# Delta-rule mixer: a head's transposes, norms and decayed keys become a step of their own, called right behind the head's projections

## The chip, the cores and the metric

The kernel runs on one core of a Trainium2 chip. The metric is the device time of one execution in microseconds (us). The engines are named as the profile names them: PE is TensorE, DVE is VectorE, ACT is ScalarE, POOL is GpSimd, SP is SyncE, whose queue issues nearly all DMAs. Each engine runs its own instructions in a fixed order. An instruction that waits for another engine holds up everything behind it on its own engine.

## The reference

Two model blocks run one after the other on 512 tokens of width 1024. The change lies in the first block's mixer, which has a gated delta rule (4 heads of 128) beside a retention (4 heads of 128). For each delta-rule head the reference computes:

```
qkv = silu(causal_dwconv(concat(q, k, v), conv_w))     # 4 taps
q, k = l2norm(q) * d**-0.5, l2norm(k)                  # per token
beta = sigmoid(b);  g = -exp(a_log) * softplus(a + dt_bias);  gcum = cumsum(g) in a chunk
m = tril(kb @ k.T * decay, -1);  t_mat = inverse(I + m);  qk = q @ k.T * decay
u = t_mat @ vb - (t_mat @ (kb * exp(gcum))) @ state
o = (q * exp(gcum)) @ state + qk @ u
state = state * exp(gcum[-1]) + (k * exp(gcum[-1] - gcum)).T @ u
out = rms(o) * norm_w * silu(gate)
```

The rest of the program is an MLP with a convolution, a window attention, an MLP, a differential attention and an MLP.

## The kernel before

All matrices are held with features on the partitions and the 512 tokens on the free axis. A projection gives one 128x512 tile: weights and activations are split into two fp32r halves, and each of the 8 slices of the contraction takes three matmuls (xh x hi, xl x hi, xh x lo), so a tile has 24 matmuls of 128x512 (`project`, PSUM buffers `ps_pj`, 3 of them). The weights come in blocks of 1 MB on SP's queue. ACT makes the high half of a block (L251), DVE the low half (L252); each half has four buffers. All other PSUM tiles share five buffers (`pwt`).

In the mixer, `conv_silu` takes a projected tile from PSUM to `cs` (DVE L556, times the row norm), starts the convolution on ACT (`cy`, L558), adds three taps on DVE (L560) and applies silu on ACT (L562) into `kT`, `KQ[:, 1]` or `vT`. The buffers of `cy` are a pair that is shared with `er` below.

`stage_a(hh)` prepares one head. Its first half makes the token-major copies of k and q by four PE transposes each (`ps_kt`), takes eight squares with a sum on ACT (`junk`, `ssq`), runs `col_rsqrt` (twelve small DVE instructions, three rounds of Newton, L400 to L410), and scales the result (`rkq`, `brk`, `kdc`). Its second half broadcasts `brk` by eight small matmuls (`ps_bc`), multiplies k by it (`KQ[:, 0]`, L590), forms the decay (`ps_gr`, then `E` on DVE, exp to `E` and `er` on ACT, four POOL operations to `E`, `E2`, `qd`, `kbe`), takes the Gram matrices (`ps_gram`, then `N` and `QE` on DVE, L622), sends `N` to DRAM, makes the decayed keys `kd` from the transposed keys that still lie in PSUM (L627), and the token-major values `vb` (`ps_vt`, L634). `stage_b1` inverts the 16x16 blocks of N on DVE (`pr`, `tt`), `stage_b2` builds the whole inverse (`ps_X`, `ps_T`, `ps_U`), `stage_c` runs the recurrence over four chunks for two heads and ends with a norm (POOL L795 on `o`). `finish` transposes `o` (`ps_oT`) and applies the gate.

The order of the calls is: k and q of heads 0, 1; the decay columns; v of heads 0, 1; `stage_a(0)`, `stage_a(1)`; k and q of heads 2, 3; `stage_b1(0)`; v of heads 2, 3; rotary projections; `stage_b2(0)`, `stage_c(0)`; `stage_a(2)`, `stage_a(3)`; `stage_b1(1)`; retention; `stage_b2(1)`, `stage_c(1)`; gates. A scheduler in the kernel's framework turns the calls into one order per engine: calls in code order have priority, `early(...)` lends a stretch the priority of an earlier point, and an instruction whose inputs the scheduler holds to be late is passed by later ready ones. So PE's order mixes projections (`ps_pj`) with the small matmuls of the stages.

Of the kernel before, what the change touches and what calls it, by code (L numbers as in the profile page):

```python
# [12 lines left out]
ALU = mybir.AluOpType  # L13
# [3 lines left out]
P = 128  # L17
# [152 lines left out]
def build(nc, tc, a, out, phases=("mix", "mlp1", "A", "mlpA", "B", "mlpB")):  # L170
# [13 lines left out]
    V = nc.vector  # L184
    G = nc.gpsimd

    def mm(o, l, r, start=True, stop=True):
        return nc.tensor.matmul(o, lhsT=l, rhs=r, start=start, stop=stop)  # L188
# [20 lines left out]
    def pwt(name, shape=None):  # L209
        return pw.tile(shape or [P, T], F32, tag="w", name=name)  # L210
# [168 lines left out]
    def project(pieces, x, n=T, cols=P):  # L379

        if pre:
            return pre.pop(0)
        ps = pj.tile([P, T], F32, tag="pj", name="ps_pj")[0:cols, 0:n]
        nk = len(x)
        for k in range(nk):
            hi, lo = pieces[k // KD]
            M_["pe"] = mm3(ps, (hi[:, k % KD, 0:cols], lo[:, k % KD, 0:cols]), x[k], k == 0, k == nk - 1)
        return ps
# [7 lines left out]
    def col_rsqrt(src, n, name, bufs=None):  # L396

        n, tn = max(n, 4), n
        xe = sp.tile([P, n], F32, tag=f"nx{n}", name="nx")[:, 0:tn]
        V.tensor_scalar(out=xe, in0=src, scalar1=EPS, scalar2=None, op0=ALU.add)  # L400
        ti = sp.tile([P, n], I32, tag=f"ni{n}", name="ni")[:, 0:tn]
        V.tensor_scalar(out=ti, in0=xe.bitcast(I32), scalar1=1, scalar2=None, op0=ALU.logical_shift_right)
        y = sp.tile([P, n], F32, tag=name, name=name, bufs=bufs)[:, 0:tn]
        V.tensor_scalar(out=y.bitcast(I32), in0=ti, scalar1=-1.0, scalar2=float(0x5F3759DF),
                        op0=ALU.mult, op1=ALU.add)
        b = sp.tile([P, n], F32, tag=f"nb{n}", name="nb")[:, 0:tn]
        for _ in range(3):
            V.scalar_tensor_tensor(out=b, in0=y, scalar=-0.5, in1=y, op0=ALU.mult, op1=ALU.mult)  # L408
            V.tensor_tensor(out=b, in0=b, in1=xe, op=ALU.mult)  # L409
            V.scalar_tensor_tensor(out=y, in0=b, scalar=1.5, in1=y, op0=ALU.add, op1=ALU.mult)  # L410
        return y
# [7 lines left out]
    def bcast(colap4):  # L419

        ps = pwt("ps_bc")
        for c in range(4):
            mm(ps[:, c * P:(c + 1) * P], colap4[:, c:c + 1].to_broadcast([P, P]), ident)
        return ps
# [50 lines left out]
    def mixer(st):  # L475
# [6 lines left out]
        NL = 32  # L482

        def unit(tag, bufs, name, dt=F32, shape=None):
            pool = lp if tag == "L" else gp
            return pool.tile(shape or [P, T], dt, tag=tag, name=name, bufs=bufs)
# [76 lines left out]

        HD = [dict() for _ in range(4)]

        def stage_a(hh):
            H = HD[hh]
            kT, KQ, vT = H["kT"], H["KQ"], H["vT"]

            ssq = sp.tile([P, 8], F32, tag="ssq", name="ssq")  # L570
            for o, src in ((0, kT), (4, KQ[:, 1, :])):
                ps = pwt("ps_kt")
                for c in range(4):
                    nc.tensor.transpose(ps[:, c * P:(c + 1) * P], src[:, c * P:(c + 1) * P], ident)
                for c in range(4):
                    junk = gp.tile([P, P], F32, tag="junk", name="junk", bufs=1)
                    act(out=junk, in_=ps[:, c * P:(c + 1) * P], func=AF.Square, accum_out=ssq[:, o + c:o + c + 1])
                if o == 0:
                    ps_k = ps
            rkq = col_rsqrt(ssq, 8, "rkq", bufs=4)  # L580
            rk, rq = rkq[:, 0:4], rkq[:, 4:8]
            V.tensor_scalar(out=rq, in0=rq, scalar1=128 ** -0.5, scalar2=None, op0=ALU.mult)
            H["rq"] = rq
            brk = sp.tile([P, 4], F32, tag="brk", name="brk")
            V.tensor_tensor(out=brk, in0=rk, in1=GT["beta"][:, :, hh], op=ALU.mult)
            kdc = sp.tile([P, 4], F32, tag="kdc", name="kdc")
            V.tensor_tensor(out=kdc, in0=rk, in1=GT["dkd"][:, :, hh], op=ALU.mult)

            ps = bcast(brk)
            V.tensor_tensor(out=KQ[:, 0, :], in0=ps, in1=kT, op=ALU.mult)  # L590
            psr = pwt("ps_gr")
            for c in range(4):
                mm(psr[:, c * P:(c + 1) * P], GT["g"][:, c, hh:hh + 1].to_broadcast([P, P]), tri)
            E = unit("L", NL, "E")
            for c in range(4):
                V.scalar_tensor_tensor(out=E[:, c * P:(c + 1) * P], in0=psr[:, c * P:(c + 1) * P],
                                       scalar=GT["gc"][:, c, hh:hh + 1], in1=mneg, op0=ALU.subtract, op1=ALU.add)
            act(out=E, in_=E, func=AF.Exp)
            er = unit("y", 2, "er")
            act(out=er, in_=psr, func=AF.Exp)  # L600
            Ev = E.rearrange("p (c i) -> p c i", c=4)
            G.tensor_tensor(out=Ev, in0=Ev, in1=rk.unsqueeze(2).to_broadcast([P, 4, P]), op=ALU.mult)
            E2 = unit("L", NL, "E2")
            E2v = E2.rearrange("p (c i) -> p c i", c=4)
            G.tensor_tensor(out=E2v, in0=Ev, in1=nstr.unsqueeze(1).to_broadcast([P, 4, P]), op=ALU.mult)
            qd = unit("L", NL, "qd")
            G.tensor_tensor(out=qd, in0=KQ[:, 1, :], in1=er, op=ALU.mult)
            H["qd"] = qd
            kbe = unit("L", NL, "kbe")
            G.tensor_tensor(out=kbe, in0=KQ[:, 0, :], in1=er, op=ALU.mult)  # L610
            H["kbe"] = kbe
            N = unit("L", NL, "N")
            QE = unit("L", NL, "QE")
            for c2 in range(2):
                ps = pwt("ps_gram")
                pg = ps.rearrange("p (c a i) -> p c a i", c=2, a=2)
                for c in range(2):
                    cc = slice((2 * c2 + c) * P, (2 * c2 + c + 1) * P)
                    mm(pg[:, c], kT[:, cc], KQ[:, :, cc])
                cs = slice(c2 * 256, c2 * 256 + 256)  # L620
                for aa, (o_, m_) in enumerate(((N, E2), (QE, E))):
                    V.tensor_tensor(out=o_[:, cs].rearrange("p (c i) -> p c i", c=2), in0=pg[:, :, aa, :],  # L622
                                    in1=m_[:, cs].rearrange("p (c i) -> p c i", c=2), op=ALU.mult)
            H["N"], H["QE"] = N, QE
            nc.sync.dma_start(d1[hh], N.rearrange("p (c i) -> p c i", c=4))
            t = unit("L", NL, "kd")
            V.tensor_tensor(out=t.rearrange("p (c d) -> p c d", c=4), in0=ps_k.rearrange("p (c d) -> p c d", c=4),  # L627
                            in1=kdc.unsqueeze(2).to_broadcast([P, 4, P]), op=ALU.mult)
            H["kd"] = t
            ps = pwt("ps_vt")  # L630
            for c in range(4):
                nc.tensor.transpose(ps[:, c * P:(c + 1) * P], vT[:, c * P:(c + 1) * P], ident)
            t = unit("L", NL, "vb")
            V.tensor_tensor(out=t.rearrange("p (c d) -> p c d", c=4), in0=ps.rearrange("p (c d) -> p c d", c=4),  # L634
                            in1=GT["beta"][:, :, hh:hh + 1].to_broadcast([P, 4, P]), op=ALU.mult)
            H["vb"] = t
# [160 lines left out]
        def gdn_proj(hp, nms):  # L797
            for (ci, nm) in ((4, "k"), (0, "q"), (8, "v")):
                if nm not in nms:
                    continue  # L800
                w = [None] * 2 if pre else ws.take()
                for i in range(2):
                    hh = 2 * hp + i
                    H = HD[hh]
                    ps = project(w[i:i + 1], x)
                    if nm == "k":
                        H["kT"] = unit("L", NL, "kT")
                        dst = H["kT"]
                    elif nm == "q":
                        H["KQ"] = unit("KQ", 2, "KQ", shape=[P, 2, T])  # L810
                        dst = H["KQ"][:, 1, :]
                    else:
                        H["vT"] = unit("L", NL, "vT")
                        dst = H["vT"]
                    conv_silu(ps, ci + hh, dst)
# [84 lines left out]
        gdn_proj(0, "kq")  # L900
        decay_cols()
        gdn_proj(0, "v")
        stage_a(0)
        stage_a(1)
        gdn_proj(1, "kq")
        stage_b1(0, M_["dve"])
        gdn_proj(1, "v")
        p0 = tc.cur_priority
# [693 lines left out]
```

## Time and profile before

| | |
|---|---|
| three runs, median | 1921.40, 1927.18, 1923.35; 1923.35 us |
| profiled execution, its own time | 1921.55 us |
| its span, first to last instruction | 1919.7 us |
| mean granted clock of PE | 0.997 |
| busy: PE, DVE, ACT, POOL | 98%, 58%, 40%, 7% |

The span leaves 1.85 us of the execution's own time outside. In a timeline, a row gives the start in the span, the duration, the engine, the line, the operation with output and inputs, and in brackets the idle time ahead of it with the instruction that ended it. Matmuls are pipelined, so the start of the next one, not the end of this one, gives a matmul's cost.

### The profile page before, as it was taken

The page shows a single profiled execution, that of the slowest core. Times are in us where ns is not written, and L with a number is a line of the kernel's source. Part 1 is how long each engine was busy: PE and PEld are TensorE (multiplying, and loading weights), DVE is VectorE, ACT ScalarE, POOL GpSimd, SP SyncE. Part 2 cuts the span into 40 slices and gives each one's busy share as a digit, 9 for nine tenths or more (in the row PEclk, how much of TensorE's full clock was granted, in tenths as well). Part 3 has the DMA queues.
Part 4 walks back from the last instruction along what each step waited for, and adds up shares of the span by engine and source line. Part 5 has one row for each costly group of instructions (what it writes and reads, how often), then busy time and mean ns, then how long its engine had stood idle before and what let it go on. Part 6 is the DMA issues. An engine that isn't in the chain of part 4 may idle for free.

```text
span 1919.7 us, 23518 instructions
## 1 busy us (share of the span) xinstructions
PE 1885.3 (98%) x9219; PEld 1545.1 (80%) x9219; DVE 1109.8 (58%) x2109; ACT 766.1 (40%) x1350; POOL 143.3 (7%) x136
## 2 busy tenths in 40 slices
PE   7999999999999999999999999999999999999997
PEld 5887878788888887777888888888888888888886
DVE  7795756666356575558544344447877754334433
ACT  5523334343234444345342133336656543213322
POOL 1231210011001002000000000001111000000000
PEclk9999999999999999999999999999999999999999
DMA  5231213222322234112323222333222232222321
GB/s 191 79 116 56 74 45 121 95 88 88 110 103 86 76 112 160 64 52 99 110 89 109 88 106 92 111 131 135 95 73 101 81 112 88 97 101 89 109 88 44
DMA packets 39646, 185.53 MB, mean 97 GB/s; under 512 B 9055, under 2 KB 10847, under 8 KB 22000
## 3 DMA queue, kind: packets, MB, share of 16 engines
q1 hardware_dynamic: 37552, 177.45, 26.3%
q0 software_dynamic: 1984, 6.59, 1.0%
q8 instruction: 72, 1.18, 0.2%
q14 instruction: 38, 0.31, 0.1%
HBM read 176.31 MB, written 7.71 MB: 96 GB/s over the span
## 4 chain that ended last, share of the span: by engine, by line
PE 55%; DVE 3%; ACT 1%; issue 1%; DVEq 0%; ACTq 0%
PE ps_pj L188 49%; PE ps_ob L188 1%; PE ps_lgb L188 1%; PE ps_po L188 1%; PE ps_aT L1380 1%; PE ps_lg L188 1%; ACT junk L1397 0%; PE ps_bc L188 0%; DVE KL L1337 0%; DVE lo L252 0%; DVE nb L408 0%; DVE nb L409 0%; PE ps_obT L1409 0%; PE ps_pT L1140 0%; PE ps_mean L188 0%
## 5 line engine op out<-in xcount | busy, mean ns | idle before, releaser
L188 PE MATMUL ps_pj<-xh,hi 128*128 128x512 f32 x1504 | 592.2, 394 | 10.2 <-ACT hi L251 9.3
L188 PE MATMUL ps_pj<-xl,hi 128*128 128x512 f32 x1504 | 591.7, 393 | 0.0
L188 PE MATMUL ps_pj<-xh,lo 128*128 128x512 f32 x1504 | 590.9, 393 | 0.0
L251 ACT ACTIVATE hi<-raw 128x1024 fp32r<-128x1024 f32 (+2 forms) x308 | 317.2, 1031 | 649.1 <-PE ps_pj L188 611.0
L252 DVE TENSOR_TENSOR lo<-raw,hi 128x1024 fp32r<-128x1024 f32 (+2 forms) x308 | 369.6, 1202 | 300.2 <-ACT hi L251 299.2
L188 PEld LDWEIGHTS ps_pj<-xh,hi 128*128 128x128 f32 x1504 | 283.1, 188 | 69.0 <-ACT hi L251 9.8
L188 PEld LDWEIGHTS ps_pj<-xh,lo 128*128 128x128 f32 x1504 | 283.1, 188 | 58.1 <-DVE lo L252 1.1
L188 PEld LDWEIGHTS ps_pj<-xl,hi 128*128 128x128 f32 x1504 | 283.1, 188 | 57.6 <-DVE xl L280 0.6
L188 PE MATMUL ps_pj<-ah,lo 128*128 128x512 f32 (+1 forms) x704 | 271.0, 385 | 0.0
L188 PE MATMUL ps_pj<-al,hi 128*128 128x512 f32 (+1 forms) x704 | 270.7, 385 | 0.2 <-DVE al L277 0.2
L188 PE MATMUL ps_pj<-ah,hi 128*128 128x512 f32 (+1 forms) x704 | 270.9, 385 | 0.0
L188 PEld LDWEIGHTS ps_pj<-al,hi 128*128 128x128 f32 x704 | 132.3, 188 | 26.9 <-DVE al L277 0.5
L188 PEld LDWEIGHTS ps_pj<-ah,hi 128*128 128x128 f32 x704 | 132.3, 188 | 26.4 <-ACT ah L276 0.4
L188 PEld LDWEIGHTS ps_pj<-ah,lo 128*128 128x128 f32 x704 | 132.3, 188 | 25.9
L469 DVE TENSOR_TENSOR ot<-ps_pj,r 128x512 f32<-128x512 f32 x31 | 21.5, 692 | 108.1 <-PE ps_pj L188 108.1
L188 PE MATMUL ps_pj<-mh,hi 128*128 128x512 f32 x192 | 74.9, 394 | 1.0 <-ACT mh L276 0.9
L276 ACT ACTIVATE ah<-ms 128x512 fp32r<-128x512 f32 x64 | 40.4, 632 | 87.4 <-DVE ms L974 85.9
L188 PE MATMUL ps_pj<-ml,hi 128*128 128x512 f32 x192 | 74.4, 392 | 0.6 <-DVE ml L277 0.6
L188 PE MATMUL ps_pj<-mh,lo 128*128 128x512 f32 x192 | 74.0, 390 | 0.0
L277 DVE TENSOR_TENSOR al<-ms,ah 128x512 fp32r<-128x512 f32 x64 | 44.3, 693 | 45.0 <-ACT ah L276 45.0
L947 DVE SCALAR_TENSOR_TENSOR my<-ms,cols,my 128x511 f32<-128x511 f32 (+1 forms) x88 | 65.6, 748 | 2.8 <-ACT my L945 1.3
L1364 ACT ACTIVATE Lb<-Lb,bmn 128x512 f32<-128x512 f32 x64 | 45.6, 714 | 13.9 <-DVE bmn L1362 11.6
(341 smaller groups left out, 1895.9 us busy)
## 6 DMA issues: line engine op xcount, KB each, us to landing
raw<-w_all SPq DMA_DIRECT2D x137, 1024.0 KB
bt<-biasd SPq DMA_DIRECT2D x16, 448.0 KB
raw<-w_all SPq DMA_DIRECT2D x8, 768.0 KB
raw<-w_all SPq DMA_DIRECT2D x8, 640.0 KB
hscr<-h POOLq DMA_DIRECT2D x16, 256.0 KB, 2.5
hold<-hscr SPq DMA_DIRECT2D x16, 256.0 KB
hs<-x_t SPq DMA_DIRECT2D x8, 256.0 KB
hold<-x_t SPq DMA_DIRECT2D x8, 256.0 KB
```

Of the source, the lines that this page charges most:

```text
L188: return nc.tensor.matmul(o, lhsT=l, rhs=r, start=start, stop=stop)
L251: act(out=hv, in_=iv, func=AF.Copy)
L252: i_lo = V.tensor_tensor(out=lv, in0=iv, in1=hv.bitcast(F32), op=ALU.subtract)
L276: act(out=dst_hi, in_=src, func=AF.Copy)
L277: V.tensor_tensor(out=dst_lo, in0=src, in1=dst_hi.bitcast(F32), op=ALU.subtract)
L469: V.tensor_tensor(out=t, in0=ps, in1=scale_row, op=ALU.mult)
L947: V.scalar_tensor_tensor(out=y[:, jj:], in0=s[:, :T - jj], scalar=col(base + m), in1=y[:, jj:], op0=ALU.mult, op1=ALU.add)
L1364: act(out=L, in_=L, func=AF.Exp, scale=-1.0, bias=mn[:, j, t:t + 1], accum_out=ss[:, j, t:t + 1])
L1380: nc.tensor.transpose(ps[:, t * P:(t + 1) * P], A[t][:, kt * P:(kt + 1) * P], ident)
```

## The change

`stage_a` is cut in two. The new `stage_a0` holds the transposes, squares, norm and scales, and the decayed keys `kd`, which stood near the end of `stage_a`. `stage_a` keeps the rest. The calls are put in another order: `stage_a0` of heads 0, 1 behind their v; then k of heads 2, 3; then `stage_a` of heads 0, 1; then q of heads 2, 3; then `stage_a0` of heads 2, 3; then on as before, with `stage_a(2)` and `stage_a(3)` where they were. The arithmetic and the number of instructions are the same.

```diff
-        def stage_a(hh):
+        def stage_a0(hh):
+
             H = HD[hh]
-            kT, KQ, vT = H["kT"], H["KQ"], H["vT"]
+            kT, KQ = H["kT"], H["KQ"]
 ...
             V.tensor_tensor(out=kdc, in0=rk, in1=GT["dkd"][:, :, hh], op=ALU.mult)
+            t = unit("L", NL, "kd")
+            V.tensor_tensor(out=t.rearrange("p (c d) -> p c d", c=4), in0=ps_k.rearrange("p (c d) -> p c d", c=4),
+                            in1=kdc.unsqueeze(2).to_broadcast([P, 4, P]), op=ALU.mult)
+            H["kd"] = t
+            H["rk"], H["brk"] = rk, brk
+
+        def stage_a(hh):
+            H = HD[hh]
+            kT, KQ, vT, rk, brk = H["kT"], H["KQ"], H["vT"], H["rk"], H["brk"]
 
             ps = bcast(brk)
 ...
             nc.sync.dma_start(d1[hh], N.rearrange("p (c i) -> p c i", c=4))
-            t = unit("L", NL, "kd")
-            V.tensor_tensor(out=t.rearrange("p (c d) -> p c d", c=4), in0=ps_k.rearrange("p (c d) -> p c d", c=4),
-                            in1=kdc.unsqueeze(2).to_broadcast([P, 4, P]), op=ALU.mult)
-            H["kd"] = t
 ...
         gdn_proj(0, "v")
+        stage_a0(0)
+        stage_a0(1)
+        gdn_proj(1, "k")
         stage_a(0)
         stage_a(1)
-        gdn_proj(1, "kq")
+        gdn_proj(1, "q")
+        stage_a0(2)
+        stage_a0(3)
         stage_b1(0, M_["dve"])
         gdn_proj(1, "v")
```

PE at the end of the first recurrence (`stage_c(0)`), before. `ps_u` and `ps_o` belong to the recurrence, `ps_pj` to the retention's values; the `ps_kt` rows are head 2's transposes, and 30 projection matmuls stand between the last row here and head 2's `ps_bc`.

```order
L188 MATMUL ps_pj<-xh_173,lo 128x512
L188 MATMUL ps_u<-vb,U 128x128
L188 MATMUL ps_o<-S,qd 128x128
L574 MATMUL ps_kt<-ident,kT 128x128 x4
L574 MATMUL ps_kt<-ident,KQ 128x128 x4
L188 MATMUL ps_o<-u,QE 128x128
```

The same place on PE after the change:

```order
L188 MATMUL ps_pj<-xh_173,lo 128x512
L188 MATMUL ps_u<-vb,U 128x128
L188 MATMUL ps_o<-S,qd 128x128
L188 MATMUL ps_bc<-ident,brk 128x128 x4
L188 MATMUL ps_gr<-cg,g 128x128 x4
L188 MATMUL ps_gram<-KQ,kT 128x256 x4
L638 MATMUL ps_vt<-ident,vT 128x128 x4
L188 MATMUL ps_o<-u,QE 128x128
```

Head 2's broadcast, decay and Gram matmuls moved up to where its transposes stood; the transposes are gone from here.

PE in the projections of v of heads 2 and 3, after the change. The first rows are the end of the matmuls of head 2's v; `KQ` in the first `ps_kt` is q of head 2, `kT` is k of head 3, and the second `KQ` is q of head 3. Before the change this stretch held projections only.

```order
L188 MATMUL ps_pj<-xh_183,hi 128x512
L188 MATMUL ps_pj<-xl_184,hi 128x512
L575 MATMUL ps_kt<-ident,KQ 128x128 [waits Activation_49]
L575 MATMUL ps_kt<-ident,KQ 128x128 x3
L575 MATMUL ps_kt<-ident,kT 128x128 [waits DVE_49,PE_49]
L575 MATMUL ps_kt<-ident,kT 128x128 x3
L188 MATMUL ps_pj<-xh_183,lo 128x512
L188 MATMUL ps_pj<-xh_193,hi 128x512
L188 MATMUL ps_pj<-xl_194,hi 128x512
L188 MATMUL ps_pj<-xh_193,lo 128x512
L575 MATMUL ps_kt<-ident,KQ 128x128 [waits PE_49,Activation_49]
L575 MATMUL ps_kt<-ident,KQ 128x128 x3
```

The transposes of heads 2 and 3 moved into this stretch, and two of them wait for ACT, that is for the silu of q.

ACT ahead of that silu, before. `E` and `er` are head 1's exponentials, the first two `cy` rows start the convolutions of k of heads 2 and 3, the next two those of q, and the silus of q stand behind both silus of k.

```order
L251 ACTIVATE hi<-raw 128x1024 [waits DMAHW4_49,PE_49]
L598 ACTIVATE E<-E 128x512 [waits DVE_49]
L600 ACTIVATE er<-ps_gr 128x512
L558 ACTIVATE cy<-cs,cols 128x512 [waits Pool_49]
L558 ACTIVATE cy<-cs,cols 128x512 [waits Activation_49,Pool_49]
L251 ACTIVATE hi<-raw 128x1024 [waits PE_49]
L562 ACT_TABLE_LOAD [waits DVE_49]
L562 ACTIVATE kT<-cy 128x512 [waits Activation_49]
L562 ACTIVATE kT<-cy 128x512 [waits DVE_49,Activation_49]
L558 ACTIVATE cy<-cs,cols 128x512 [waits Activation_49] x2
L251 ACTIVATE hi<-raw 128x1024 [waits DMAHW2_49,PE_49]
L562 ACTIVATE KQ<-cy 128x512 [waits DVE_49,Activation_49] x2
```

The same on ACT after the change. The two `cy` rows are now those of q of heads 2 and 3 (those of k stand further up), and the `junk` rows are squares of head 2's transposed keys.

```order
L251 ACTIVATE hi<-raw 128x1024 [waits DMAHW4_49,PE_49]
L608 ACTIVATE E<-E 128x512 [waits DVE_49]
L610 ACTIVATE er<-ps_gr 128x512 [waits Activation_49]
L558 ACTIVATE cy<-cs,cols 128x512 [waits DVE_49,Activation_49,Pool_49]
L251 ACTIVATE hi<-raw 128x1024 [waits PE_49]
L578 ACTIVATE junk,ssq<-ps_kt 128x128 [waits PE_49]
L578 ACTIVATE junk,ssq<-ps_kt 128x128 [waits Activation_49]
L558 ACTIVATE cy<-cs,cols 128x512 [waits DVE_49,Pool_49]
L578 ACTIVATE junk,ssq<-ps_kt 128x128 [waits Activation_49]
L562 ACT_TABLE_LOAD
L562 ACTIVATE KQ<-cy 128x512 [waits DVE_49]
```

The silus of k moved ahead of the exponentials; the silu of q of head 2 stands behind the `cy` of q of head 3, which waits for DVE and POOL.

## Rows read from the trace of the kernel before

**Rows 1.** The page, part 1: busy time, share, instructions of each engine.
```profile
PE 1885.3 (98%) x9219; PEld 1545.1 (80%) x9219; DVE 1109.8 (58%) x2109; ACT 766.1 (40%) x1350; POOL 143.3 (7%) x136
```

**Rows 2.** Windows: span, length; busy PE, PEld, DVE, ACT, POOL; granted clock; DMA.
```profile
180.00:200.00 20.00, 17.65 (x85) 14.94 (x85) 13.27 (x54) 9.81 (x35) 6.91 (x6) 0.91 0.04 14
```

**Rows 3.** Timeline of PE, the second halves of `stage_a(2)` and `stage_a(3)`.
```profile
186.21 0.39 PE L188 MATMUL ps_pj<-xl,hi 128*128 128x512 f32 x1
186.44 0.39 PE L188 MATMUL ps_pj<-xh,lo 128*128 128x512 f32 x1
189.18 1.84 PE L188 MATMUL ps_bc<-ident,brk 128*128 128x128 f32 x8 [2.35 <-DVE brk L585]
...
194.43 0.60 PE L632 MATMUL ps_vt<-ident,vT 128*128 128x128 f32 x4
...
205.33 1.13 PE L188 MATMUL ps_bc<-ident,brk 128*128 128x128 f32 x8
...
209.13 0.60 PE L632 MATMUL ps_vt<-ident,vT 128*128 128x128 f32 x4
```

**Rows 4.** Timeline of DVE, the norm of head 2 ahead of `brk`.
```profile
185.58 0.17 DVE L400 TENSOR_SCALAR nx<-ssq 128x8 f32<-128x8 f32 x1
...
186.60 1.04 DVE L410 SCALAR_TENSOR_TENSOR rkq<-nb,rkq 128x8 f32<-128x8 f32 x1
```

**Rows 5.** Timeline of PE, the mixer's other waits that bear on the change.
```profile
65.49 1.13 PE L188 MATMUL ps_bc<-ident,brk 128*128 128x128 f32 x8 [0.22 <-DVE t L789]
...
80.48 1.13 PE L188 MATMUL ps_bc<-ident,brk 128*128 128x128 f32 x8 [0.40 <-DVE kdc L587]
...
241.74 1.10 PE L188 MATMUL ps_X<-T,N 128*128 128x64 f32 x8 [0.71 <-POOL T L671]
...
285.15 0.66 PE L889 MATMUL ps_oT<-ident,o 128*128 128x128 f32 x4 [0.49 <-POOL o L795]
...
287.42 0.66 PE L889 MATMUL ps_oT<-ident,o 128*128 128x128 f32 x4 [0.69 <-POOL o L795]
```

**Rows 6.** Timeline of PE, transposes of head 0.
```profile
56.06 0.60 PE L574 MATMUL ps_kt<-ident,kT 128*128 128x128 f32 x4
56.49 0.60 PE L574 MATMUL ps_kt<-ident,KQ 128*128 128x128 f32 x4
```

**Rows 7.** Timeline of ACT, first the exponential of head 0, then the convolutions of heads 2, 3.
```profile
68.71 0.63 ACT L598 ACTIVATE E<-E 128x512 f32<-128x512 f32 x1 [3.99 <-DVE E L596]
...
89.90 0.73 ACT L558 ACTIVATE cy<-cs,cols 128x512 f32<-128x512 f32 x1 [4.47 <-POOL kbe L610]
90.53 1.05 ACT L251 ACTIVATE hi<-raw 128x1024 fp32r<-128x1024 f32 x1
92.15 1.28 ACT L562 ACT_TABLE_LOAD   x1 [0.58 <-DVE cy L560]
93.44 1.27 ACT L562 ACTIVATE kT<-cy 128x512 f32<-128x512 f32 x2
...
98.85 1.29 ACT L562 ACTIVATE KQ<-cy 128x512 f32<-128x512 f32 x2 [1.96 <-DVE cy L560]
```

**Rows 8.** Timeline of POOL, `E` and `E2` of head 0, `E2` of head 1.
```profile
69.42 1.04 POOL L602 TENSOR_TENSOR E<-E,rkq 128x512 f32<-128x512 f32 x1 [35.55 <-ACT E L598]
70.53 1.29 POOL L605 TENSOR_TENSOR E<-E,cg 128x512 f32<-128x512 f32 x1
...
85.53 1.83 POOL L605 TENSOR_TENSOR E<-E,cg 128x512 f32<-128x512 f32 x1
```

**Rows 9.** Timeline of DVE behind the projection of q of head 2 (`cs` at 79.51 is its tile).
```profile
79.51 0.68 DVE L556 TENSOR_TENSOR cs<-ps_pj,rs 128x512 f32<-128x512 f32 x1
...
85.46 0.75 DVE L560 SCALAR_TENSOR_TENSOR cy<-cs,cols,cy 128x511 f32<-128x511 f32 x1 [1.79 <-ACT cy L558]
...
87.40 0.42 DVE L622 TENSOR_TENSOR N<-ps_gram,E 128x256 f32<-128x256 f32 x1 [1.18 <-POOL E L605]
...
88.73 0.68 DVE L627 TENSOR_TENSOR kd<-ps_kt,kdc 128x512 f32<-128x512 f32 x1
```

## Prediction

> **What bounds the kernel now.** I read the shares of busy time first: PE is busy for 98% of the span and every other engine for under 60% [rows 1]. So the end is set by PE's own work and by the few places where PE stands still or runs slowly. The change takes no matmul away; it can only move the places where PE waits. Next I read the windows of the mixer, from 0 to 360 us. Only one of them has a granted clock below 1.00: 0.91, with PE busy for 17.65 of 20 us [rows 2]. It is the stretch in which head 2 is prepared. Then I read PE's timeline there. PE has finished its projections and waits 2.35 us for `brk`, the last step of head 2's norm. After that pause the broadcast-to-values block, from the start of `ps_bc` to the start of `ps_vt`, takes 194.43 − 189.18 = 5.25 us, where the same block of head 3 takes 209.13 − 205.33 = 3.80 us [rows 3]. By its durations the first block starts at the lower of the two clock levels (1.2 instead of 2.4 GHz) and comes back to the upper one. So this stall costs 2.35 + 1.45 = 3.80 us. Why `brk` is late is in DVE's timeline: the norm starts at 185.58 and has twelve dependent instructions, one of which takes 1.04 us instead of 0.17 [rows 4]. The other waits that bear on the change are short: 0.22 and 0.40 us for the norms of heads 0 and 1, 0.71 us at the first `ps_X` of heads 2 and 3, 0.49 and 0.69 us at the transposes of the finished heads 2 and 3 [rows 5]. None is followed by a low clock.
>
> Behind the mixer the order of every engine is the same in both kernels, so what PE gains or loses here arrives at the end in full.
>
> **The change part by part.**
>
> *Removed.* Head 2's norm is made some 80 us ahead of its use, so neither `brk` of head 2 nor that of head 3 can be late: −3.80. What is late next at that place is the product `KQ[:, 0]`, which DVE makes between `ps_bc` and `ps_gram`; nothing heavy is queued ahead of it on DVE, and eight `ps_gr` matmuls cover it. I give it 0.2. For heads 0 and 1 both projections of k now stand between the transposes and `ps_bc`; 48 matmuls at 0.23 us [rows 3] are 11.0 us, against 9.4 us that passed from head 0's transposes at 56.06 [rows 6] to its `ps_bc` at 65.49 [rows 5]. So 0.22 + 0.40 = 0.62 goes.
>
> *The first `ps_X` of heads 2 and 3* waits for POOL, which waits for the inverse of the 16x16 blocks on DVE, which waits for head 3's `N`. Head 3's `N` now comes before the retention has started, since its transposes and its norm are gone from the path. The 0.71 goes; nothing else stands in POOL's queue ahead of it there.
>
> *The finished heads 2 and 3* (1.18 us of waits) keep the same chain of sums, norm and POOL product. Now 16 projection matmuls cover the first and 19 the second, where 30 and 4 did; but on DVE fewer evacuations stand inside the norm. The nearest rows are the two waits themselves. I take 0.7 for what stays, so 0.48 goes; the ends are 0 and 1.5.
>
> Removed in all: 3.80 + 0.62 + 0.71 + 0.48 = 5.61.
>
> *Added: the transposes of q of head 2.* PE arrives there, in the middle of head 2's v, after 24 matmuls of q of head 3, 17 of v and one group of transposes behind the end of q of head 2: 41 × 0.23 + 0.43 [rows 3, 6] = 9.86 us. They wait for the silu of that q on ACT. ACT's queue is the long way: the high half of a weight block 1.05 and the exponential of head 1 0.63 [rows 7]; then POOL's `E` 1.04 and `E2` 1.29 [rows 8]; then on DVE four `N` and `QE` products, 88.73 − 87.40 = 1.33, one 128x512 product for `vb` 0.68 (as `kd`), one tap 0.75 and the evacuation of q of head 3 0.68 [rows 9]; then on ACT the `cy` of q of head 3 0.73, a 128x128 square, for which I estimate half of the exponential's 0.63, a table load 1.28 and the silu, half of 1.27, 0.64 [rows 7]. The sum is 10.4, so the wait is 0.5 us. With `E2` at the 1.83 us that it also took [rows 8] it is 1.1. I take 1.0. The nearest rows for a wait in that kind of chain are 0.22 from below and 2.35 from above [rows 3, 5]; the upper one brings the low clock, 1.45, with it. Behind the waiting transposes PE has all its projections queued, so the wait counts in full.
>
> *The other new waits.* The transposes of q of head 3 stand five matmuls and two groups behind, and the second silu follows the first after three squares: 0.2. The first `ps_gram` of head 0 waits for a product that stands on DVE behind the convolutions of k: 0.1, at most 0.8. The transposes of the retention's values wait for one of the five shared PSUM buffers, which head 3's Gram product frees after POOL's `E2`; POOL has the norm product of head 1 in its queue near there. I take 0.4 out of 0 to 0.9. With the 0.2 for head 2's product this makes 1.0 + 0.2 + 0.1 + 0.4 + 0.2 = 1.9.
>
> *Costs nothing.* The same 16 transposes of heads 2 and 3 move (0.43 us a group of four), the 16 squares and the 24 small DVE operations of each pair move with them. They now lie beside the projections of v and of the rotary heads. There PE needs an evacuation from DVE per tile of 24 matmuls, 5.5 us, and the three PSUM buffers give each about two tiles' time. If that cover were gone, an evacuation would be late by what the two norms add on DVE, 24 × 0.17 = 4.1 us [rows 4]. The decayed keys `kd` come earlier and free their PSUM buffer earlier. SP's queue has the weights ahead of `N`'s transfers; no weight block comes near its due time.
>
> *Sum.* −5.61 + 1.9 = −3.7 us. On the profiled execution: 1921.55 − 3.7 = 1917.85. That execution lies 1.8 us below the median of the three runs, 1923.35, to which the new median is compared: 1923.35 − 3.7 = 1919.65.
>
> *A rule that speaks against it.* In the trace a table load takes 1.28 us, and the silu behind it starts at 93.44, 0.01 us after its end [rows 7]. The Trainium skill, page "ScalarE: Activation LUTs", section "What ACT_TABLE_LOAD costs", adds a drain of 1380 ns to each load. By it the wait for the silu of q would be 2.4 us, about the pause after which the clock fell, and the sum would be −3.7 + 1.38 + 1.45 = −0.9, so 1922.5. The row shows no room for a drain behind the load, so I leave it out.
>
> **The rivals.**
>
> *A: the old waits go and no new one comes.* If the silu of q is in time and the other new waits are covered, PE gains the 5.61, and with all of the 1.18 of the finished heads 6.3: 1923.35 − 6.3 = 1917.0, at the least 1917.7. For it: the wait for the silu is a difference of 0.5 between two sums of ten. Against it: five separate covers must hold.
>
> *B: the saved waits come back as new ones.* A total of new waits of 4 to 7.5 us instead of 1.9, for instance 2.35 and a low clock of 1.45 at the transposes of q, gives −2 to +2: 1921.35 to 1925.35. For it: the chain to the silu crosses four engines, and one slow product on any of them lengthens it [rows 4, 8]. The rule of the skill would end here.
>
> *C: slower, at one place.* The chain from q of head 2 to its silu takes as long as it did: its evacuation starts at 79.51 and the first of the two silus ends at 98.85 + 0.64, 20.0 us later [rows 7, 9]. PE comes 9.86 us after the projection, so it would wait 10.1 us and then run 1.45 us at the low clock; less the 1.0 that I have already, −3.7 + 10.1 + 1.45 − 1.0 = +6.9, 1930.2. It decides from a chain of 13.1 us, at which the change is worth nothing. For it: `cy` still waits for POOL's `kbe` to free its buffer, which cost 4.47 us [rows 7]. Against it: in those 20 us the convolutions and silus of both k were queued ahead, and they are now done earlier.
>
> **How the numbers follow.** The forecast, −2 to −5.7, has 0.49, A 0.21, B 0.18, C 0.12. A difference below 0.3%, 5.8 us, can't be told from none. Faster by more needs a time below 1917.6: most of A and little of the forecast's own case, 0.26. Slower by more needs 1929.1: C, 0.10. The rest, 0.64, is the same. The range reaches from 1914.5, which is A less 2.5 for the shift of a median (the three runs lie from −1.95 to +3.8 around theirs), to 1925.5, the upper end of B. It leaves out C and the tails.
>
> **What would show it.** Right: PE's `ps_bc` of head 2 has no wait, the window from 180 us has a clock of 1.00, and the blocks of heads 2 and 3 take 3.8 us. New rows are expected at the transposes of q of head 2 with a wait of about 1 us for the silu of ACT, and none above 0.5 elsewhere. The forecast is wrong if that wait is above 2.35 us with a clock below 1.00 around 95 us (B), if it is about 10 us (C), or if there is none (A); and wrong in another way if a rotary projection waits for DVE, or a new wait stands in the retention.

## The result, and the profile after

The changed kernel takes 1939.68 us, the median of five executions (1934.65 to 1940.02). The kernel before, timed again beside it, has 1923.35 us, the median of five (1921.40 to 1929.89). The ratio is 1.0066, with a 95% interval from 1.0045 to 1.0087, so the change makes the kernel slower by 0.66%. The forecast was 1919.65 us in a range that ended at 1925.5; it was wrong.

The profiled execution of the changed kernel has 1936.77 us, its span is 1934.8 us and its mean granted clock 0.989. Before it was 1921.55, 1919.7 and 0.997. I account below for the difference of the two spans, 15.1 us.

The page of the profile after: busy time, share and instructions of each engine, and PE's granted clock in 40 slices of the span. It answers to [rows 1].

```profile
PE 1897.2 (98%) x9219; PEld 1555.5 (80%) x9219; DVE 1111.0 (57%) x2109; ACT 765.6 (40%) x1350; POOL 144.0 (7%) x136
...
PEclk9999979999999999999999999999999999999999
```

The work is the same to the instruction, and DVE, ACT and POOL are as busy as before. PE is busy 11.9 us longer with the same matmuls: it runs slowly somewhere. The 7 in the sixth slice says where to look.

Windows of the kernel after: span and length, busy PE, PEld, DVE, ACT, POOL, granted clock, DMA. The first row answers to [rows 2].

```profile
180.00:200.00 20.00, 17.95 (x113) 15.35 (x112) 15.23 (x49) 7.32 (x16) 10.18 (x8) 1.00 0.15 54
...
234.90:265.62 30.72, 30.72 (x207) 24.89 (x207) 8.44 (x22) 4.76 (x14) 0.00 (x0) 0.50 0.10 35
...
360.00:365.00 5.00, 5.00 (x15) 3.25 (x14) 2.22 (x4) 0.00 (x0) 0.00 (x0) 0.66 0.18 24
```

The window from 180 us, 0.91 before, is at 1.00 now. But from 234.9 to 265.6 us, for 30.7 us, the clock stands at 0.50, its lower level (1.2 GHz), with PE busy all the time. A short dip at 361 us is new as well.

PE's waits from the start to 360 us, each with the line, what ended it, the total in us, how often, and the longest. First the kernel before:

```profile
PE ps_pj L188 <- ACT hi L251: 9.3, 2, 9.0
PE ps_bc L188 <- DVE brk L585: 2.4, 1, 2.4
PE ps_oT L889 <- POOL o L795: 1.2, 2, 0.7
...
PE ps_X L188 <- POOL T L671: 0.7, 1, 0.7
...
```

The same view of the kernel after:

```profile
PE ps_pj L188 <- ACT hi L251: 10.3, 1, 10.3
PE ps_T L188 <- DVE X L702: 1.9, 1, 1.9
PE ps_tm L436 <- DVE QE L632: 1.7, 1, 1.7
PE ps_kt L575 <- ACT KQ L562: 1.6, 1, 1.6
PE ps_oT L895 <- POOL o L801: 1.2, 2, 0.7
PE ps_gram L188 <- DVE KQ L600: 1.0, 3, 0.6
```

All the waits for the norms (`brk`, and those of 0.22 and 0.40 in [rows 5]) and the wait at `ps_X` are gone. Four places have new ones: the transposes of q (`ps_kt`), the Gram products, the transposes of the retention's values (`ps_tm`), and, the longest, `ps_T`. The first row is PE's wait for the first weights at the start of the program; it has nothing to do with the change, but it makes 1.0 us of the difference.

Timeline of PE after: start, duration, engine, line, operation with output and inputs, idle time ahead of it and what ended that. The first rows answer to [rows 3], the last ones stand at the first `ps_X` of heads 2 and 3, which [rows 5] showed with a wait of 0.71.

```profile
183.38 1.06 PE L188 MATMUL ps_bc<-ident,brk 128*128 128x128 f32 x8
...
185.49 1.99 PE L188 MATMUL ps_gram<-KQ,kT 128*128 128x256 f32 x8 [0.17 <-DVE KQ L600]
187.32 0.60 PE L638 MATMUL ps_vt<-ident,vT 128*128 128x128 f32 x4
...
231.03 1.00 PE L188 MATMUL ps_X<-T,N 128*128 128x64 f32 x8
...
234.68 1.74 PE L188 MATMUL ps_T<-X,U 128*128 128x64 f32 x8 [1.89 <-DVE X L702]
236.21 1.92 PE L188 MATMUL ps_U<-U,X 128*128 128x64 f32 x8
237.91 1.91 PE L188 MATMUL ps_X<-T,N 128*128 128x64 f32 x8
```

Head 2's block from `ps_bc` to `ps_vt` now takes 187.32 − 183.38 = 3.94 us, against 5.25 [rows 3], and nothing waits ahead of it. At 231.03 `ps_X` no longer waits for POOL. But 3.65 us later `ps_T` has waited 1.89 us for DVE's `X`. Eight such matmuls then take 1.74 us, and in the groups behind 1.9 us, instead of 1.0: that is the lower clock.

Why `X` is late is in DVE's timeline, from the end of the norm of the retention's head 2 to that of its head 3, the last one. It answers to [rows 4].

```profile
225.16 1.29 DVE L410 SCALAR_TENSOR_TENSOR fc<-nb,fc 128x4 f32<-128x4 f32 x1
...
227.10 0.62 DVE L400 TENSOR_SCALAR nx<-rss 128x4 f32<-128x4 f32 x1
227.75 1.22 DVE L402 TENSOR_SCALAR ni<-nx 128x4 int32<-128x4 int32 x1
229.00 1.21 DVE L404 TENSOR_SCALAR fc<-ni 128x4 int32<-128x4 int32 x1
230.25 0.16 DVE L408 SCALAR_TENSOR_TENSOR nb<-fc 128x4 f32<-128x4 f32 x1
...
233.51 0.69 DVE L877 TENSOR_TENSOR ro<-ps_ro,fc 128x512 f32<-128x512 f32 x1
234.11 0.41 DVE L702 TENSOR_TENSOR X<-ps_X,cg 128x256 f32<-128x256 f32 x1
```

And POOL's timeline of the same time, the first and the last of its four products `T` and `U` of heads 2 and 3, which run without a gap, each of 1.28 to 1.30 us:

```profile
225.15 1.29 POOL L677 TENSOR_TENSOR T<-cmp,cg 128x512 f32<-128x512 f32 x1
...
228.91 1.28 POOL L677 TENSOR_TENSOR U<-cmp,cg 128x512 f32<-128x512 f32 x1
```

The two are read side by side. A step of the norm takes 0.16 us when POOL is idle; while POOL runs its products four of them end almost together with a product each, at 226.45, 227.72, 228.97 and 230.21. They took 4.34 us instead of 0.66, 3.7 us longer, and the `ro` behind the norm and the `X` behind that on DVE's queue are late. How late is measured by `r1_pool_late` below, 2.7 us: without the products the norm would have waited for ACT for a part of the time. In the kernel before, the first of the products came some 15 us later, and one step of the norm lay beside them:

```profile
239.72 1.98 POOL L671 TENSOR_TENSOR T<-cmp,cg 128x512 f32<-128x512 f32 x1 [4.69 <-DMA cmp<-d]
...
240.48 1.23 DVE L410 SCALAR_TENSOR_TENSOR fc<-nb,fc 128x4 f32<-128x4 f32 x1
```

**The account of the 15.1 us.** Before the change sets in, PE is 1.0 us late by the first weights (the first `ps_kt` starts at 57.05 instead of 56.06 [rows 6]). The rest is read at `ps_mean`, the first small matmuls behind the mixer, first in the kernel before, then after, then in the second experiment below (`r2_fill`), whose mixer has the change's order on PE and no low clock:

```profile
340.02 1.02 PE L188 MATMUL ps_mean<-inv_d,acc 128*128 128x1 f32 x8
353.63 1.02 PE L188 MATMUL ps_mean<-inv_d,acc 128*128 128x1 f32 x8
340.32 1.02 PE L188 MATMUL ps_mean<-inv_d,acc 128*128 128x1 f32 x8
```

So the change is 13.6 us late there, 12.6 of them made in the mixer, and the remaining 1.5 come behind it: the dip at 361 us, a little over three microseconds at half clock. The low clock is sized by `r2_fill`: its `ps_mean` starts 13.3 us ahead of that of the change, its first `ps_T` 0.3 us ahead, so the low clock costs 13.0. Beside it stand the waits. Gone: 3.80 for `brk` with its low clock, 0.62 for heads 0 and 1, 0.71 at `ps_X`: −5.13. New among projections: 1.61 + 1.66 + 0.56 + 0.17 + 0.23 = +4.23. The pause at `ps_T`: +1.89. With the low clock this makes +14.0 for the mixer, 1.4 more than the 12.6 measured. So PE gained about 1.4 us that is in none of these terms: 0.2 is a second wait of `ps_T` for ACT's `X`, which is gone; the rest stands in no wait of the lists, and where it lies is open.

### The profile page after: what moved, and what is told of

It is laid out like the page before. It is cut to its first block, busy times and chain, and to the rows that moved or that the text cites. A ratio compares the mean times of both kernels' runs of the same rounds, so it can differ in the third digit from the quotient of the medians.

```text
span 1934.8 us, 23503 instructions
## 1 busy us (share of the span) xinstructions
PE 1897.2 (98%) x9219; PEld 1555.5 (80%) x9219; DVE 1111.0 (57%) x2109; ACT 765.6 (40%) x1350; POOL 144.0 (7%) x136
## 3 DMA queue, kind: packets, MB, share of 16 engines
q8 instruction: 72, 1.18, 0.2%
## 4 chain that ended last, share of the span: by engine, by line
PE 55%; DVE 3%; ACT 1%; issue 1%; DVEq 0%; ACTq 0%
PE ps_pj L188 49%; PE ps_ob L188 1%; PE ps_lgb L188 1%; PE ps_po L188 1%; PE ps_aT L1391 1%; PE ps_lg L188 1%; ACT junk L1408 0%; DVE lo L252 0%; PE ps_bc L188 0%; DVE KL L1348 0%; DVE nb L408 0%; DVE nb L409 0%; PE ps_obT L1420 0%; PE ps_pT L1151 0%; PE ps_mean L188 0%
## 5 line engine op out<-in xcount | busy, mean ns | idle before, releaser
L954 DVE TENSOR_TENSOR ms<-ps_pj,rs 128x512 f32<-128x512 f32 x44 | 30.2, 687 | 37.2 <-PE ps_pj L188 37.2
```

The lines of the kernel that those rows point to most:

```text
L954: V.tensor_tensor(out=s, in0=ps, in1=st.rs, op=ALU.mult)
```

## The experiments

Two theories stood against each other. Theory 1: POOL's products beside the norm make `X` late, PE pauses, and the pause at the edge of the stretch of small matmuls (`stage_b2(1)`, called the thin stretch below) brings the low clock for its whole length. Theory 2: the pause is not needed; the thin stretch has fewer projections among its small matmuls than before, and the clock falls there by itself. Each experiment is timed against the kernel before on the same chip. That kernel had medians of 1927.85 (29 executions), 1927.17 (35) and 1928.09 (17) in the three groups in which the experiments were run.

**r1_pool_late: POOL's products kept behind the norm.** A small product that needs the last `ro` stands ahead of `T` and `U` on POOL; its output is not used.

```diff
+ g0 = G.tensor_tensor(out=gx, in0=after_g[:, 0:4], in1=after_g[:, 4:8], op=ALU.mult)
...
+ in_order(g0, gt_)        # gt_: each product T, U
- stage_b2(1, None, pe1)
+ stage_b2(1, R[3]["o"], pe1)
```

> The changed kernel with one small POOL product put ahead of T and U of heads 2 and 3, which waits for the norm of the last retention head; POOL's four products of 1.3 us then no longer lie beside that norm. Theory 1 (a pause of PE at the first ps_T of heads 2 and 3, made by POOL slowing the norm on DVE, lets the clock fall): DVE's steps of that norm take about 0.2 us each again, the idle time of 1.89 us at ps_T is under 0.7, the granted clock from 240 to 260 us is above 0.9, and the time is 11 to 14 us below the changed kernel. Theory 2 (the clock falls because the stretch of small matmuls comes behind other waits, or by itself, and the pause is only beside it): the clock stays at 0.5 there and the time falls by 2 us at most.

Measured: 1947.58 us, ratio 1.0086 [1.0058, 1.0114]. The steps of the norm took 0.16 to 0.17 us again. DVE's timeline, the start of the last norm and the last `ro`:

```profile
227.98 0.17 DVE L400 TENSOR_SCALAR nx<-rss 128x4 f32<-128x4 f32 x1 [0.91 <-ACT junk L878]
...
231.85 0.69 DVE L882 TENSOR_TENSOR ro<-ps_ro,fc 128x512 f32<-128x512 f32 x1
```

Ahead of this norm DVE is 1.0 us later than in the changed kernel (an earlier `ro` starts at 222.20 instead of 221.19), so 231.85 against 233.51 means 2.7 us sooner, more than the pause of 1.89: the first half of theory 1 holds. But the pause only moved. PE's timeline:

```profile
234.08 1.11 PE L188 MATMUL ps_X<-T,N 128*128 128x64 f32 x8 [1.22 <-POOL T L680]
```

and the window behind it:

```profile
240.00:260.00 20.00, 19.89 (x167) 15.51 (x167) 6.23 (x15) 2.92 (x8) 0.00 (x0) 0.50 0.17 54
```

`ps_X` now waits 1.22 us for POOL's `T`, and the clock falls as before. So this run does not tell the theories apart. Its time is also 8 us above that of the change itself: in some stretches its projections start 233 ns apart instead of 227 (500 to 540 us: 173 instructions instead of 178, at a granted clock of 1.00). I have no cause for that. One of its eight executions has a mean clock of 0.997, which leaves no room for such a low stretch, and still takes 1939.24 us.

**r2_fill: the pause filled.** The first `ps_X` of heads 2 and 3 is computed three times, so that PE works while `X` is on its way; the result is the same.

```diff
- for c in range(4):
+ for c in range(4 * (3 if hp == 1 and i == 0 else 1)):
+     c = c % 4
```

> The changed kernel with the eight matmuls of the first ps_X of heads 2 and 3 run three times over (the same result), about 1.6 us of work in place of the idle time; nothing else moves. Theory 1: DVE's steps stay slow (1.2 us each beside POOL), but PE's idle time at ps_T is 0.5 us or less, the clock from 240 to 260 us is above 0.9 and the time 11 to 14 us below the changed kernel. Theory 2: the clock is 0.5 there all the same and the time stays within 1 us of the changed kernel.

Measured: 1923.05 us, ratio 0.9973 [0.9954, 0.9993]. PE's timeline and a window:

```profile
230.76 2.79 PE L188 MATMUL ps_X<-T,N 128*128 128x64 f32 x24
...
234.38 1.08 PE L188 MATMUL ps_T<-X,U 128*128 128x64 f32 x8
```

```profile
240.00:260.00 20.00, 20.00 (x207) 15.29 (x204) 10.20 (x26) 8.12 (x22) 0.00 (x0) 1.00 0.15 54
```

With the same projections in the thin stretch as the change has, and 16 more matmuls of 64 columns (1.8 us) ahead of it, the clock stays at 1.00 and the profiled execution ends 13.5 us ahead of that of the change (1936.77 − 1923.27). That is against theory 2 as the main cause. This execution has a short low clock of its own far behind the mixer:

```profile
891.00:895.00 4.00, 4.00 (x24) 2.79 (x23) 3.97 (x8) 2.21 (x4) 0.00 (x0) 0.58 0.00 0
```

Its span is 1.6 us longer than that of the kernel before, and only 0.3 us of that stand at `ps_mean`.

**r3_pause and r3_half: the pause alone, in the kernel before.** `X` is evacuated seven times (four in `r3_half`) instead of once, with PE's order held; the result is the same.

```diff
- V.tensor_tensor(out=cols_of(X, 0).rearrange(...), ...)
+ for _ in range(7 if hp == 1 and i == 0 else 1):
+     V.tensor_tensor(out=cols_of(X, 0).rearrange(...), ...)
```

> The kernel before, with DVE's evacuation X of the first ps_X of heads 2 and 3 done seven times over (the same result), and PE's order held as it was: PE gets an idle time of 2.0 to 2.5 us at ps_T, where it had none. Theory 1: the granted clock falls to 0.5 behind it for 20 to 30 us and the kernel is 12 to 16 us slower than before. Theory 2: no low clock behind it, 2 to 3 us slower.

> The kernel before with DVE's evacuation X of the first ps_X of heads 2 and 3 done four times over and PE's order held: a pause of about 1.3 us at ps_T instead of 2.6. Theory 1, after the run in which a pause of 1.22 us at ps_X was enough: the clock falls to 0.5 all the same, 11 to 14 us slower than before. If a pause must be longer than the 1.66 us that did no harm elsewhere: no low clock, 1.5 us slower.

Measured: 1939.95 us, 1.0059 [1.0035, 1.0083], with seven, and 1935.59 us, 1.0048 [1.0022, 1.0075], with four: 12.1 and 8.4 us above the kernel before in their groups, the second less than the 11 to 14 expected. `r3_pause`, PE's timeline and a window:

```profile
248.22 1.94 PE L188 MATMUL ps_T<-X,U 128*128 128x64 f32 x8 [2.68 <-DVE X L709]
```

```profile
246.96:277.68 30.72, 29.34 (x198) 23.31 (x199) 8.11 (x21) 3.81 (x11) 0.34 (x1) 0.50 0.10 35
```

`r3_half`, the same:

```profile
250.82 1.94 PE L188 MATMUL ps_T<-X,U 128*128 128x64 f32 x8 [1.29 <-DVE X L709]
```

```profile
250.61:281.33 30.72, 30.40 (x203) 24.36 (x204) 7.42 (x20) 3.81 (x11) 0.66 (x1) 0.50 0.10 35
```

In both the clock falls while PE stands still. Nothing of the change is in these kernels but a late `X`, and a pause of 1.29 us is followed by 30.7 us at the lower clock. All 18 executions have a mean clock of 0.992 or less, where the kernel before has that in 16 of 64. The pause alone brings the loss: theory 1. (The profiled execution of `r3_half`, 1941.69 us, has a low clock in the first thin stretch too, as in `b_look2` below.)

**r4_heads23 and r5_heads01: one pair of heads alone.** `r4_heads23` calls `stage_a0` and `stage_a` of heads 0 and 1 as before and only `stage_a0(2)`, `stage_a0(3)` early; `r5_heads01` keeps heads 2 and 3 as before.

```diff
  stage_a0(0)                      # r4_heads23
- stage_a0(1)
- gdn_proj(1, "k")
  stage_a(0)
+ stage_a0(1)
  stage_a(1)
- gdn_proj(1, "q")
+ gdn_proj(1, "kq")
```

> The change for heads 2 and 3 alone: their transposes, norms and kd behind their projections, heads 0 and 1 in the order of before. Theory 1: the retention still starts early, POOL's T and U still lie beside the last norm, the pause and the low clock from 235 to 265 us come, and the time is within 4 us of the changed kernel. If the loss came from the new order of heads 0 and 1, the time is within 3 us of the kernel before.

> The change for heads 0 and 1 alone: k of heads 2 and 3 stands between the transposes and the rest, and the transposes and norms of heads 2 and 3 stay with the rest of their step, late. Theory 1: the wait of 2.35 us for brk of head 2 stays, the retention starts late, POOL's T and U come behind the last retention norm, no low clock behind 235 us; within 3 us of the kernel before. If the new order of heads 0 and 1 had a part in the low clock, it is 8 us or more slower than before.

Measured: `r4_heads23` 1936.60 us, 1.0036 [1.0014, 1.0059], with the same pause (1.88 us for `X` at 233.83) and the clock at 0.50 from 240 to 260 us. Heads 2 and 3 are the part that does it. The waits at the transposes of heads 2 and 3 are 0.54 + 0.22 us instead of 1.61; the rest comes with heads 0 and 1. `r5_heads01` took 1935.12 us, 1.0037 [1.0008, 1.0065], which I had not expected. Its profiled execution, at 1922.75 us its fastest, shows no low clock behind a pause of 1.31 us. PE's timeline and window:

```profile
243.32 1.10 PE L188 MATMUL ps_X<-T,N 128*128 128x64 f32 x8 [1.31 <-POOL T L677]
```

```profile
240.00:260.00 20.00, 18.49 (x210) 14.46 (x209) 7.69 (x18) 3.17 (x8) 4.92 (x4) 1.00 0.18 57
```

Seven of its ten executions had a mean clock of 0.992 or less; none of them was profiled, so where those lose is not shown. A pause of 1.2 to 1.3 us at this place is followed by the low clock in some kernels or executions (`r1_pool_late`, `r3_half`) and not in others, and no bound for it can be read from these runs.

**m1_hold: projections in place of the repeated product.** Nine projection matmuls more are held between the first `ps_X` and `ps_T`, so nothing is computed twice.

```diff
+ M_["hold"] = [2, ti]              # ti: the first ps_T of head 2
...
+ in_order(M_["pe"], M_["hold"][1])
```

> The changed kernel with nine more of the projection matmuls, which run later anyway, held ahead of the first ps_T of heads 2 and 3 (12 between ps_X and ps_T instead of 3). Nothing is computed twice. Theory 1 (the pause ahead of the thin stretch lets the clock fall): no idle time above 0.3 us at ps_T, clock 1.00 from 240 to 260 us, and 4 us below the kernel before, like the run with the matmuls repeated. Theory 2 (the repeated matmuls helped because they added work to the stretch, not because they closed the pause): the clock falls in the stretch, since its later part has nine projections fewer, and the kernel stays above the kernel before.

Measured: 1926.49 us, ratio 0.9995 [0.9976, 1.0014]. That is no better than the kernel before, where I had expected 4 us less. The pause is gone, but the projections held there are missing later, and the clock fell from 246.3 to 256.5 us. A window of its profile:

```profile
246.30:256.54 10.24, 10.24 (x49) 7.99 (x48) 2.79 (x9) 2.73 (x7) 0.00 (x0) 0.50 0.01 2
```

PE did not stand still there; the fall comes in a group of 64x64 matmuls (`ps_X`, from 245.74), right behind a group of 32x32 ones. So theory 2 has a part: the clock can fall in the thin stretch with no pause ahead of it, here for 10 us instead of 31.

**m4_all: the other new waits moved too.** `m1_hold`, with `stage_a0(2)` and `stage_a0(3)` behind v of heads 2 and 3, and nine projection matmuls ahead of the third `ps_tm`.

```diff
- stage_a0(2)
- stage_a0(3)
  stage_b1(0, M_["dve"])
  gdn_proj(1, "v")
+ stage_a0(2)
+ stage_a0(3)
```

> As the run before it, and two further waits taken away in the same manner: the transposes of heads 2 and 3 stand behind their projections of v (not in the middle), and nine projection matmuls are held ahead of the third transpose of the retention's values. If the waits of 1.61 us for the silu of q and of 1.66 us at that transpose go and none takes their place, it is 2.5 to 3.3 us below the run before it, 7 below the kernel before. If the pause only moves, it is the same as the run before it.

Measured: 1929.34 us, ratio 1.0014 [0.9991, 1.0037]. The transposes of q wait no more, but a rotary projection waits 3.1 us for DVE's `rqk` and `ps_tm` 1.4 us for DVE's `vs`: the waits came back elsewhere. So the expected gain over `m1_hold` did not come. In its profile the clock is 0.58 from 160 to 180 us, in the other thin stretch (`stage_b2(0)`).

**r6_best: heads 2 and 3 alone, with the pause filled.** The edits of `r4_heads23` and `r2_fill` together.

> The change for heads 2 and 3 alone (heads 0 and 1 in the order of before), with the first ps_X of heads 2 and 3 run three times over as in the earlier run. Theory 1: no pause at ps_T, clock 1.00 from 230 to 265 us, 5 to 6 us below the kernel before, about 1 us below the changed kernel with the same filling, since the wait at the transposes of q of head 2 is 0.6 us or less. Theory 2 (the low clock has to do with the move of heads 2 and 3 and not with the pause): the clock falls to 0.5 there and it is 8 us or more slower than before.

Measured: 1922.32 us, ratio 0.9964 [0.9945, 0.9983]. This is below the kernel before by the ratio, but see the next run on what the ratio means. In its profiled execution, at 1929.66 us its slowest, the clock is 1.00 from 220 to 300 us and fell in the first thin stretch.

**b_look1, b_look2, b_look3: the kernel before, unchanged, profiled three times.** In the timings the kernel before did not stay at one time, and its mean clock went along.

> The kernel before, unchanged, profiled once more: its times on this chip fall into groups around 1922, 1927.5 and 1935 us with mean clocks of 0.997, 0.994 and 0.990. Theory 1: an execution of one of the upper groups shows a granted clock of 0.5 for 10 us or more between 240 and 275 us, behind a pause at the first ps_X or in the stretch of small matmuls behind it; one of the lowest group shows none. Theory 2 (the groups are another matter): the clock is 1.00 there in all groups and is low elsewhere.

> The kernel before, unchanged, once more, with the expectations of the run before it; which of the groups the profiled execution falls into is chance.

> The kernel before, unchanged, a third time, with the same expectations; which of the groups the profiled execution falls into is chance.

Measured: 1922.26 us with a mean clock of 0.997, and 1928.15 and 1928.50 with 0.994. A window of `b_look1` in the first thin stretch:

```profile
159.40:173.05 13.65, 13.65 (x104) 10.20 (x102) 6.84 (x20) 3.96 (x15) 0.00 (x0) 1.00 0.00 1
```

and of `b_look2`:

```profile
159.40:173.05 13.65, 13.65 (x69) 10.15 (x68) 3.87 (x10) 1.87 (x8) 0.00 (x0) 0.50 0.00 0
```

The same program, with no wait above 0.2 us at that place, loses about 6 us in one execution and not in another. I had looked for it in the second thin stretch; it is the first. In the three groups of timings 28 of 81 executions of the kernel before had a clock above 0.996 (medians 1921.87, 1922.32 and 1922.01 us), 32 about 0.994 (near 1928) and 21 about 0.990 (near 1935). The last kind was met in no profile, so where those lose is open.

This also corrects how the ratios of `r2_fill` and `r6_best` are read. With a mean clock above 0.996 they take 1922.74 (7 of 10) and 1922.15 us (10 of 12), and the kernel before takes 1921.87 and 1922.01 beside them. At that clock there is no gain. Their ratios below 1 come from executions at a lower clock being rarer, 3 of 10 against 20 of 29 and 2 of 12 against 13 of 17. Why they are rarer was not tested.

## Why the prediction was wrong

**The step that failed** is that on the first `ps_X` of heads 2 and 3: "The 0.71 goes; nothing else stands in POOL's queue ahead of it there." The 0.71 went, for the reason given: POOL's products came early. What they would lie beside in their new place was not asked, and the wait behind them was put at nothing. They lie beside the retention's last norm on DVE, which stands ahead of `X`, and PE waits 1.89 us for `X` instead of 0.71 for `T`. With the 13.0 us of low clock behind it this is 14.9 us that the sum did not have, and `r2_fill` takes the low clock away with the pause. [rows 4] held the warning, a step of 1.04 us among those of 0.17, and I read it only as a reason why `brk` was late.

The Trainium skill, page "SBUF — State Buffer", section "Who interferes with whom", says that a DVE instruction with two inputs in SBUF contends with a GpSimd instruction that reads SBUF, that one in a two-port mode, which `tensor_scalar` can enter, contends with GpSimd too, and that the one that issues second stands still for the other's whole instruction. The trace agrees: L410, with two inputs, took 1.29 us beside a product of 1.29, and L402 and L404, which are `tensor_scalar`, 1.22 and 1.21. Which mode those two ran in no trace shows.

**The price of a pause.** I priced every new wait at its own length, and a long one at 1.45 us of low clock on top, from [rows 2, 3]. That price was of a pause with full projections behind it. This one stands at the edge of the thin stretch, and the clock came back only 31 us later: 13.0 us, nine times 1.45. `r2_fill` and `r3_pause` show it from both sides. Rival C had the sign and another place; its wait of 10.1 us at the transposes of q did not come, and 1.61 us did.

**The removed waits** were right: the 3.80 went with its low clock, the 0.62 and the 0.71 went. Only the 0.48 at the finished heads did not (0.70 + 0.51 = 1.21 us now, 1.18 before).

**The new waits were too small.** The transposes of q: 1.61 us instead of 1.0 + 0.2. The chain in which the silu of q stands, from the timelines of POOL, DVE and ACT after:

```profile
85.83 1.56 POOL L612 TENSOR_TENSOR E<-E,rkq 128x512 f32<-128x512 f32 x1 [2.10 <-DMA inst<-d]
87.47 1.62 POOL L615 TENSOR_TENSOR E<-E,cg 128x512 f32<-128x512 f32 x1
...
91.05 1.08 DVE L560 SCALAR_TENSOR_TENSOR cy<-cs,cols,cy 128x510 f32<-128x510 f32 x1
...
92.83 0.73 ACT L558 ACTIVATE cy<-cs,cols 128x512 f32<-128x512 f32 x1 [1.47 <-DVE cs L556]
...
93.62 0.19 ACT L578 ACTIVATION_READ_ACCUMULATOR junk<-ps_kt 128x1 f32 x1
93.82 1.28 ACT L562 ACT_TABLE_LOAD   x1
95.12 0.63 ACT L562 ACTIVATE KQ<-cy 128x512 f32<-128x512 f32 x1
```

What I had undersized lies ahead of `cy`: POOL's `E` and `E2` took 1.56 and 1.62 us instead of the 1.04 and 1.29 of the sum, and DVE's tap 1.08 instead of 0.75. The load has no gap ahead of it and none behind it. So the 1380 ns of drain that the Trainium skill (page "ScalarE: Activation LUTs", section "What ACT_TABLE_LOAD costs") adds don't show as a separate time. `ps_tm`: 1.66 instead of 0.4, outside the bounds that I gave (0 to 0.9). The Gram products: 0.56 + 0.17 + 0.23 instead of 0.1 + 0.2. In all 4.23 instead of 1.9. By these waits the sum without the pause would be −5.13 + 4.23 = −0.9 and not −3.7, the end of rival B.

PE's own rows say something else. From head 0's transposes (56.70 in `r2_fill`, 56.06 before) to `ps_mean`, `r2_fill` takes 283.62 us and the kernel before 283.96. Without the 1.8 us of repeated matmuls that is −2.1, so some 1.2 us of gain lie in no term of that sum, as in the account above. Without the pause the change would have ended at the edge of the forecast's −2 to −5.7, and that partly by luck. In the timings, at a mean clock above 0.996, the median of `r2_fill` lies 0.87 us above that of the kernel before (1922.74 and 1921.87), where these rows would put it 0.3 below; the low clock at 891 us would be enough for that, but whether it came in all these executions is not shown.

**The forecast's own test** named the failure, "or a new wait stands in the retention", as a way of being wrong, and gave it no time and no chance. That is where the range went wrong.

## What to carry to other kernels

A wait of PE is priced by what stands behind it: among full projections 1.6 us cost 1.6 us, at the edge of a stretch of small dependent matmuls 1.9 us cost 14.9 with the low clock behind it. When work is moved earlier, write down for every engine what it now runs beside, and look above all for a chain of small DVE steps beside a POOL product. If such a pause can't be taken away, a few matmuls of filling in it may be cheaper than the pause, and kernels with stretches of small matmuls should be profiled more than once, since the clock there differs between executions.

## What the runs showed of the hardware

- Four DVE steps of 128x4, 0.16 us each, took 4.34 us beside POOL products of 1.29 us; each ended with one of the products.
- Pauses of 1.22, 1.29, 1.89 and 2.68 us at the edge of the thin stretch were followed by a granted clock of 0.50 for 27 to 31 us; one of 1.31 us there was not, in the one execution profiled, nor were pauses of 1.61 and 1.66 us among projections.
- The clock also fell with no pause of PE above 0.2 us, in or just behind groups of 64x64 matmuls that follow 32x32 ones: for 10 us in `m1_hold`, and from 159.4 to 173 us in two of the four profiles of the kernel before, alike but for that. What decides it is open.
- So is the dip at 361 us after the change. It begins near the end of eight 33x16 matmuls (`ps_bias`), and `r1_pool_late`, `m1_hold` and `r6_best` show it at the same place of the program (a clock of 0.66 in five microseconds); the four profiles of the kernel before, `r2_fill` and `r4_heads23` do not.
